# Gate and branch projections moved behind the attention as four stages of seven block products

## The chip, the cores and the metric

The kernel runs on one core of a Trainium2 chip. Its engines have instruction queues of their own: TensorE (PE, with its weight loads PEld), VectorE (DVE), ScalarE (ACT), GpSimd (POOL), and SyncE (SP), which issues most transfers. They meet through semaphores. The metric is the device time of one execution in microseconds, as the median of several runs.

## The reference

One layer on x of 1024 tokens by 1024 channels, in float32. A modulated RMS norm gives h; one combined projection of h feeds two attention branches and the merging gates.

```python
h = rms_norm(x, norm_w[l]) * (1.0 + scale) + shift
hq, hf, hi, hz, gq, gk, gv, gz, ga, mg = jnp.split(h @ w_in[l], IN_OFFSETS, axis=-1)
y_h = hgrn2_branch(hq, hf, hi, hz, ...)   # 8 heads, gated linear attention, rms norm, * silu(hz)
y_g = gla_branch(gq, gk, gv, gz, ga, ...) # 4 heads, the same with other gates
u_h = y_h @ w_branch[l, 0]
u_g = y_g @ w_branch[l, 1]
mg = jax.nn.sigmoid(mg.reshape(B, T, N_BRANCH, D_MODEL))
merged = mg[:, :, 0] * u_h + mg[:, :, 1] * u_g
x = x + gate * (merged @ w_out[l])
return rms_norm(x, final_norm_w)
```

The two halves of `mg`, `u_h` and `u_g` are four products of 1024 x 1024 by 1024 x 1024. They are what the change touches.

## The kernel before

Activations lie transposed, channels on the partitions and the 1024 tokens along the free axis, as eight tiles. For a float32 result every operand is split into two float32r parts, hi and lo, and every product is the sum hi*hi + hi*lo + lo*hi (`split`, L155 on ScalarE and L158 on VectorE). Buffers are 46 slots of 4 KB per partition, given out in program order.

The dense work is a list of jobs. A `Feat` (L422) makes one tile of 128 features for all tokens: 8 channel tiles x 3 parts x 2 token halves = 48 matmuls of 512 columns (`mm_feat`, L414), into one PSUM tile `pd` of 1024 columns; two such tiles take turns. A `Vblk` (L440) makes 256 value features in token layout with 256-column matmuls (L473 to L475). The jobs run in this order: the GLA branch's tiles; then `mg` for u_g and u_g itself (16 Feats; the gated result goes to DRAM, `t1_dram`, L886); the HGRN2 branch's tiles; then `mg` for u_h and u_h itself (16 Feats; L1014 fetches t1 again, L1022 to L1027 multiply and add); then the output projection in token layout (`OutBlk`, L1078 to L1080).

The attention of a head is a generator (`attention`, L487) woven into the jobs. It does a step (small matmuls on TensorE, products of decays on VectorE, copies on ScalarE) and yields the number of dense units, one about six 512-column matmuls, that are to run before its next step. Its score matmuls are L511, L543, L572, L579 and L585, into the PSUM tile `sc_ps`; between them VectorE scales q and k by decays (L591, L592). A root mean over a head or a branch (`root_mean`) sums squares on GpSimd (L791, L965), splits the sum and multiplies it with ones (L769, L770). `Stream.go` runs the jobs and counts units; where a branch product needs a head that is not through, it runs the woven work to its end (`jobs_done`).

After the opening, a list scheduler settles the order within each engine from the program's order. GpSimd issues few transfers, SP the rest.

## Time and profile before

| | |
|---|---|
| median of 3 runs | 1288.39 us (1286.5 to 1289.18) |
| span of the profiled execution | 1287.7 us; the page gives no other time of its own for it |
| TensorE busy | 1254.3 us, 97% |
| VectorE, ScalarE, GpSimd busy | 659.9, 408.8, 89.1 us |
| matmuls (rows) | 9179, of which 3168 are L414 |
| moved by DMA | 86.00 MB, mean 67 GB/s |
| TensorE on the chain that ended last | 61% |

The span is what one execution took from its first to its last instruction. A matmul's row is longer than its share of the time, since the next one starts while it drains; the price of one is read from the starts of neighbours. "Idle before" names what an engine stood still for.

### The profile page before, as it was taken

The page shows a single profiled execution, that of the slowest core. Times are in us where ns is not written, and L with a number is a line of the kernel's source. Part 1 is how long each engine was busy: PE and PEld are TensorE (multiplying, and loading weights), DVE is VectorE, ACT ScalarE, POOL GpSimd, SP SyncE. Part 2 cuts the span into 40 slices and gives each one's busy share as a digit, 9 for nine tenths or more (in the row PEclk, how much of TensorE's full clock was granted, in tenths as well). Part 3 has the DMA queues.
Part 4 walks back from the last instruction along what each step waited for, and adds up shares of the span by engine and source line. Part 5 has one row for each costly group of instructions (what it writes and reads, how often), then busy time and mean ns, then how long its engine had stood idle before and what let it go on. Part 6 is the DMA issues. An engine that isn't in the chain of part 4 may idle for free.

```text
span 1287.7 us, 20979 instructions
## 1 busy us (share of the span) xinstructions
PE 1254.3 (97%) x9179; PEld 1059.2 (82%) x9179; DVE 659.9 (51%) x1053; ACT 408.8 (32%) x606; POOL 89.1 (7%) x104
## 2 busy tenths in 40 slices
PE   4899999999999999999999999999999999999997
PEld 3767889889898888888889879888988888878886
DVE  5736334563837362224564556375466430585534
ACT  4566712333223241112232332333233231222222
POOL 5500000000000000000000000000000000140000
PEclk9799999999999999999999999999999999999999
DMA  8613010202002103363010201020010111333302
GB/s 273 224 33 90 26 34 2 66 2 66 18 19 65 34 17 115 122 211 92 18 34 18 82 2 34 17 83 18 18 50 18 50 50 50 131 98 130 132 33 99
DMA packets 99822, 86.00 MB, mean 67 GB/s; under 512 B 3211, under 2 KB 89281, under 8 KB 99730
## 3 DMA queue, kind: packets, MB, share of 16 engines
q1 hardware_dynamic: 98242, 80.24, 20.2%
q0 software_dynamic: 1440, 4.40, 0.9%
q8 instruction: 72, 1.18, 0.4%
q14 instruction: 20, 0.16, 0.0%
q10 hardware_dynamic: 48, 0.01, 0.0%
HBM read 76.25 MB, written 8.39 MB: 66 GB/s over the span
## 4 chain that ended last, share of the span: by engine, by line
PE 61%; DVE 2%; issue 0%; POOL 0%; ACT 0%; POOLq 0%; DVEq 0%; ACTq 0%
PE pd L414 41%; PE pd L473 2%; PE pd L474 2%; PE pd L475 2%; PE pd L1080 2%; PE pd L1079 2%; PE pd L1078 2%; PE pm L657 1%; PE pm L659 1%; PE pm L640 1%; PE sc_ps L511 1%; PE sc_ps L543 1%; PE pm L621 0%; DVE b L158 0%; PE sc_ps L572 0%
## 5 line engine op out<-in xcount | busy, mean ns | idle before, releaser
L414 PE MATMUL pd<-b,b 128*128 128x512 f32 x3168 | 750.1, 393 | 1.7 <-DVE b L1026 1.7
L414 PEld LDWEIGHTS pd<-b,b 128*128 128x128 f32 x3168 | 587.4, 188 | 125.9 <-DVE b L1026 2.1
L158 DVE TENSOR_TENSOR b<-b,b 128x1024 fp32r<-128x1024 f32 (+1 forms) x143 | 171.8, 1216 | 191.9 <-ACT b L155 112.5
L155 ACT CAST b<-b 128x1024 fp32r<-128x1024 f32 (+1 forms) x143 | 134.6, 955 | 302.8 <-PE pd L414 86.3
L473 PE MATMUL pd<-b,b 128*128 128x256 f32 x512 | 149.6, 292 | 0.0
L475 PE MATMUL pd<-b,b 128*128 128x256 f32 x512 | 144.9, 283 | 0.0
L474 PE MATMUL pd<-b,b 128*128 128x256 f32 x512 | 144.8, 283 | 0.0
L473 PEld LDWEIGHTS pd<-b,b 128*128 128x128 f32 x512 | 98.0, 191 | 1.4
L474 PEld LDWEIGHTS pd<-b,b 128*128 128x128 f32 x512 | 98.1, 192 | 0.5
L475 PEld LDWEIGHTS pd<-b,b 128*128 128x128 f32 x512 | 98.0, 191 | 0.0
L591 DVE TENSOR_TENSOR b<-b,tot 128x512 f32<-128x512 f32 x36 | 24.8, 690 | 71.3 <-PE sc_ps L572 27.5
L1078 PE MATMUL pd<-b,b 128*128 128x512 f32 x128 | 49.8, 389 | 0.0
L1079 PE MATMUL pd<-b,b 128*128 128x512 f32 x128 | 49.8, 389 | 0.0
L1080 PE MATMUL pd<-b,b 128*128 128x512 f32 x128 | 49.8, 389 | 0.0
L965 POOL TENSOR_TENSOR b<-b,b 128x1024 f32<-128x1024 f32 x7 | 17.5, 2495 | 464.8 <-ACT b L954 464.8
L758 ACT ACTIVATE b<-pd 128x1024 f32<-128x1024 f32 x24 | 24.6, 1026 | 73.7 <-PE pd L414 73.7
L657 PE MATMUL pm<-scT,b 128*128 128x128 f32 x256 | 46.8, 274 | 0.0
L646 DVE SCALAR_TENSOR_TENSOR b<-b,tot,pm 128x128 f32<-128x128 f32 (+1 forms) x72 | 28.2, 391 | 31.9 <-PE pm L640 30.3
L659 PE MATMUL pm<-b,b 128*128 128x128 f32 x224 | 43.3, 275 | 0.0
L657 PEld LDWEIGHTS pm<-scT,b 128*128 128x128 f32 x256 | 39.2, 191 | 1.7
L855 ACT ACTIVATE b<-pd 128x1024 f32<-128x1024 f32 x16 | 16.4, 1026 | 73.9 <-PE pd L414 73.9
L759 DVE TENSOR_TENSOR b<-b,pd 128x1024 f32<-128x1024 f32 x24 | 29.2, 1218 | 18.8 <-ACT b L758 18.8
(191 smaller groups left out, 1264.2 us busy)
## 6 DMA issues: line engine op xcount, KB each, us to landing
b<-in_w_in_dram SPq DMA_DIRECT2D x66, 512.0 KB, 3.7
b<-in_x_dram SPq DMA_DIRECT2D x16, 512.0 KB, 5.6
b<-in_ada_w_dram SPq DMA_DIRECT2D x32, 256.0 KB, 5.9
b<-in_w_branch_dram SPq DMA_DIRECT2D x16, 512.0 KB, 4.1
t_dram<-b POOLq DMA_DIRECT2D x8, 512.0 KB, 3.6
b<-in_ada_w_dram SPq DMA_DIRECT2D x8, 512.0 KB, 5.4
b<-t_dram SPq DMA_DIRECT2D x8, 512.0 KB, 4.4
b<-in_w_out_dram SPq DMA_DIRECT2D x8, 512.0 KB, 4.6
```

Source lines behind the costliest of these rows:

```text
L155: i = nc.scalar.copy(hi, src)
L158: (eng or nc.vector).tensor_sub(lo, src, hi.bitcast(F32))
L414: nc.tensor.matmul(ps[0:w, th * 512:(th + 1) * 512], a[:, k, 0:w], b[:, th * 512:(th + 1) * 512], start=(k == 0 and n == 0), stop=(k == KT ...
L473: nc.tensor.matmul(o, lh, hi[:, k % 4, :], start=(k == 0), stop=False)
L474: nc.tensor.matmul(o, lh, lo[:, k % 4, :], start=False, stop=False)
L475: nc.tensor.matmul(o, ll, hi[:, k % 4, :], start=False, stop=(k == KT - 1))
L657: nc.tensor.matmul(o, vch(ch)[:, vh * P:(vh + 1) * P], scT[:, ch, :], start=True, stop=(ch == 0))
L659: nc.tensor.matmul(o, state(ch)[:, vh * P:(vh + 1) * P], q[:, ch * P:(ch + 1) * P], start=False, stop=True)
L759: nc.vector.tensor_mul(s, s, ps)
L1078: nc.tensor.matmul(po, lh, hi[:, k % 2, :], start=(k == 0), stop=False)
L1079: nc.tensor.matmul(po, lh, lo[:, k % 2, :], start=False, stop=False)
L1080: nc.tensor.matmul(po, ll, hi[:, k % 2, :], start=False, stop=(k == KT - 1))
```

## The change

The 32 Feats of the gates and the branches leave the job list. GLA and HGRN2 jobs follow each other, and behind the last of them stand four stages: the gate of u_g, the gate of u_h, u_g and u_h. Each is a product of 1024 x 1024 matrices, worked in *pairs* of neighbouring feature tiles. For a pair, the weights are a 2 x 2 block matrix (channel halves by the two tiles) and the activations another (channel halves by token halves). Its four output blocks come from seven block products instead of eight, by Strassen's scheme in a form that reuses sums. A block product is 4 channel tiles x 3 parts = 12 matmuls of 512 columns (L1242 of the changed kernel). Each stage runs the products in the order 1, 2, 5, 6, 3, 7, 4, each for its four pairs, so a product's activation factor is loaded once per stage; the second stage uses the first one's factors.

The sums and differences that the scheme needs are made beforehand, while the attention runs, and kept in DRAM: of the activations by `factors` (VectorE, L1087), of the weights by `weight_sums` (VectorE, L1118 to L1122), both stored by GpSimd's queue. They run on a second woven track (`back`); the first track's pace is 1.1 steps of attention per unit instead of 1. h, y_g and y_h go to DRAM as well (`put_act`, L227).

Within a pair, partial results stay in PSUM where they can. After a product, ScalarE or VectorE reads the bank: a snapshot into SBUF (L1218, L1220), a finished block (L1229, or the gate's and branch's own step: L1315, L1320 sigmoid, L1330, L1337 product), or ScalarE writes an earlier snapshot into a bank on which the next product accumulates (L1225). The banks are the six 512-column halves of the two `pd` tiles and of `sc_ps`, which is lent when the last head's scores are through (`scores_done`). The last stage adds the stored u_g part with an accumulating DMA (L1340), and `make_m` splits the result for the output projection, which now starts with tokens 512 to 1023.

```diff
-ROOM = 9
-LOOK = 6
+PACE = 1.1
+PRODUCTS = (1, 2, 5, 6, 3, 7, 4)
+SUMS = {5: 0, 6: 1, 3: 2, 7: 3}
+SEEDS = {(6, 2): 0, (6, 3): 1, (3, 0): 2, (3, 1): 3}
...
     def make_h(half, d):
...
+        if d % 2:
+            nc.gpsimd.dma_start(h_d[half][d // 2], hT[half, d // 2].rearrange("p a t -> p (a t)"))
...
         def weave(self, units):
-            entry = self.side[0]
-            entry[1] -= units
...
+            for track, pace in ((self.side, PACE), (self.back, 1)):
+                if not track:
+                    continue
+                entry = track[0]
+                entry[1] -= units * pace
...
+    def put_act(acts, d, y):
+        for half in range(2):
+            nc.gpsimd.dma_start(acts[half][d // 2][:, d % 2 * 512:d % 2 * 512 + 512], y[:, half * 512:half * 512 + 512])
+        S.free(y)
...
-    for d in range(LOOK):
-        J.append(Feat(col(C_MG + D + d * P), rhs_h, mg_done(gate1, d)))
-    for d in range(8):
-        J.append(Feat(w_branch[0, 1, :, d * P:(d + 1) * P], rhs_yg, ug_done(d)))
-        if d + LOOK < 8:
-            J.append(Feat(col(C_MG + D + (d + LOOK) * P), rhs_h, mg_done(gate1, d + LOOK)))
...
-    for d in range(8):
-        J.append(Feat(col(C_MG + d * P), rhs_h, mg0_done(d)))
-    for d in range(8):
-        J.append(Feat(w_branch[0, 0, :, d * P:(d + 1) * P], rhs_yh, uh_done(d)))
...
+    def factors(acts, f, mul=None):
+        sub = nc.vector.tensor_sub
+        for kk in range(2):
...
+            for p, dst, a, b in ((5, "11", "12", "11"), (7, "12", "12", "22"), (6, "22", "22", "11"), (4, "21", "21", "22")):
+                sub(y[dst], y[a], y[b])
+                nc.gpsimd.dma_start(f[p][kk], y[dst])
...
+    def weight_sums(b, i):
...
+        add(parts[7], x1[:, :, 0], x1[:, :, 1])
+        add(parts[5], x1[:, :, 1], x2[:, :, 1])
+        yield 1.5
+        add(parts[6], parts[7], x2[:, :, 1])
+        add(parts[3], parts[6], x2[:, :, 0])
...
+        def run(self, p):
+            if p in (1, 5):
+                self.bank[BANK[p]] = R.get()
+            o = self.bank[BANK[p]]
...
+            for kt in range(4):
+                h_hi, h_lo = (z[kt // 2][:, kt % 2, :] for z in h)
+                sl = slice(kt * P, (kt + 1) * P)
+                for n, (a, c) in enumerate(((hi, h_hi), (hi, h_lo), (lo, h_hi))):
+                    nc.tensor.matmul(o, a[:, sl], c, start=(p in (1, 5) and kt == 0 and n == 0),
+                                     stop=(kt == 3 and n == 2), skip_group_check=True)
...
+        def after(self, p):
+            bank, snap, out = self.bank, self.snap, outs[self.b]
+            if p == 1:
+                snap[1] = self.snap_of("a", -1.0)
+            elif p == 2:
+                out(2 * self.i, 0, bank["a"], False)
+                R.free(bank.pop("a"))
+            elif p == 5:
+                snap[5] = self.snap_of("e")
+                R.free(bank.pop("e"))
+                self.seed("b", snap[1])
+                Q.free(snap.pop(1))
+            elif p == 6:
+                snap[6] = self.snap_of("b", -1.0)
+            elif p == 3:
+                self.summed(0, 1, None, bank["e"], ALU.subtract, 6)
+                R.free(bank.pop("e"))
+            elif p == 7:
+                self.summed(1, 1, bank["b"], None, ALU.add, 5)
+            else:
+                out(2 * self.i + 1, 0, bank["b"], False)
+                R.free(bank.pop("b"))
...
+    def put_m(d, half, ap, summed):
+        sl = slice(half * 512, half * 512 + 512)
+        g = gate0[d][:, sl]
+        nc.vector.tensor_mul(g, g, ap)
+        if summed:
+            Q.free(ap)
+        nc.gpsimd.dma_start(g, gate1[d][:, sl], accum_op=ALU.add)
+        later.append((d, half))
...
     stream.go()
+    S.free(*h_hi, *h_lo)
+    for _ in range(2):
+        pd = dtile()
+        R.lend([pd[:, 0:512], pd[:, 512:1024]])
+    last_stages()
+    make_m()
+    out0.run({1: out1.load, 3: out1.prep})
+    out1.run({})
```

Below, (b, p) names product p of stage b, b from 0 to 3. Three places show how the order moved. On TensorE, between two branch tiles of u_h before (the numbers tell buffers apart; `x2` is the same weights on both token halves):

```order
L414 MATMUL pd_9326<-b_9032,b_9283 128x512 x2
L414 MATMUL pd_9326<-b_9033,b_9283 128x512 x2
L414 MATMUL pd_9326<-b_9032,b_9284 128x512 x2
L414 MATMUL pd_9394<-b_5319,b_9351 128x512 [waits DVE_49,Activation_49]
L414 MATMUL pd_9394<-b_5320,b_9351 128x512 x2
L414 MATMUL pd_9394<-b_5319,b_9352 128x512 x2
```

and in the second stage after, at product (1, 2), where `pd_7871` and `pd_7872` are the two 1024-column tiles, each with two pairs' banks:

```order
L1242 MATMUL pd_7871<-b_7892,b_8735 128x512
L1242 MATMUL pd_7871<-b_7894,b_8735 128x512
L1242 MATMUL pd_7871<-b_7892,b_8736 128x512
L1242 MATMUL pd_7872<-b_8078,b_8771 128x512 [waits Activation_49]
L1242 MATMUL pd_7872<-b_8080,b_8771 128x512
L1242 MATMUL pd_7872<-b_8078,b_8772 128x512 [waits DVE_49]
L1242 MATMUL pd_7872<-b_8078,b_8771 128x512
L1242 MATMUL pd_7871<-b_7891,b_8735 128x512 [waits Activation_49]
L1242 MATMUL pd_7871<-b_7893,b_8735 128x512
```

Before, a tile is read once, after 48 matmuls, while the next 48 fill the other tile. Now a bank is read after 12; four matmuls of another pair stand between the end of one half of `pd_7871` and the start of its other half, which waits for ScalarE's read.

On VectorE, in the fourth GLA head between the steps L572, L579 and L585, before:

```order
L591 TENSOR_TENSOR b_608<-b_608,tot_744 128x32x16
L592 TENSOR_TENSOR b_2628<-b_2628,tot_744 128x32x16
L598 COPY_PREDICATED blk<-mask_735,sc_ps 128x8x16
L591 TENSOR_TENSOR b_608<-b_608,tot_744 128x16x32
L592 TENSOR_TENSOR b_2628<-b_2628,tot_744 128x16x32
L591 TENSOR_TENSOR b_608<-b_608,tot_744 128x8x64
L592 TENSOR_TENSOR b_2628<-b_2628,tot_744 128x8x64
```

and after, where L634 and L635 are the former L591 and L592:

```order
L634 TENSOR_TENSOR b_636<-b_636,tot_776 128x32x16
L635 TENSOR_TENSOR b_2889<-b_2889,tot_776 128x32x16
L641 COPY_PREDICATED blk<-mask_767,sc_ps 128x8x16
L196 TENSOR_TENSOR b_4029<-b_3850,b_4028 128x1024
L1118 TENSOR_TENSOR b_4050<-b_3969 128x512
L1119 TENSOR_TENSOR b_4049<-b_3969,b_3970 128x512
L634 TENSOR_TENSOR b_636<-b_636,tot_776 128x16x32
L635 TENSOR_TENSOR b_2889<-b_2889,tot_776 128x16x32
L1121 TENSOR_TENSOR b_4049<-b_4050,b_3970 128x512
```

Two weight sums and a subtraction of a weight split came between the updates of q and k that TensorE's next scores need.

On ScalarE, while u_h is made before (L155 casts weights, 1024 columns, or the merged result, 512 columns):

```order
L155 CAST b_9419<-b_9324 128x1024 [waits DMAHW2_49]
L155 CAST b_9246<-b_8708 128x512 [waits DVE_49,Pool_49]
L155 CAST b_9246<-b_8708 128x512 [waits DVE_49]
L155 CAST b_9314<-b_8793 128x512 [waits DVE_49,PE_49,Pool_49]
L155 CAST b_9314<-b_8793 128x512 [waits DVE_49]
```

and around products (3, 7) and (3, 4) after (L193 casts the merged result, L1182 weights, L1163 activation factors; DMASW are the transfers that GpSimd issues, here the accumulating ones):

```order
L1220 ACTIVATE b_10060<-sc_ps 128x512 [waits PE_49]
L1225 COPY sc_ps<-b_9937 128x512 [waits Activation_49]
L1225 COPY pd_7872<-b_9980 128x512 [waits DVE_49]
L1225 COPY sc_ps<-b_9980 128x512 [waits DVE_49]
L193 CAST b_9897<-b_8753 128x512 [waits DMASW3_49]
L1182 CAST b_10237<-b_10139 128x1024 [waits DMAHW3_49,DMAHW2_49,PE_49]
L193 CAST b_9915<-b_8769 128x512 [waits DMASW4_49]
L1182 CAST b_10188<-b_10085 128x1024 [waits DMAHW1_49,PE_49]
```

The casts of the merged result waited for VectorE; now they wait for a transfer, with weight casts behind them in ScalarE's queue, and between them stand the reads and seeds of PSUM banks.

More of the change, by code (lines that the diff above doesn't have):

```diff
@@ L691, in go @@
         def go(self, loads=2, preps=1):
+            n = len(self.jobs)
             for i, job in enumerate(self.jobs):
@@ new lines, in half_of, with put_gate1 @@
+    def half_of(store, d, half):
+        if d not in store:
+            store[d] = S.get([T])
+        return store[d][:, half * 512:half * 512 + 512]
+    gate0, gate1 = {}, {}
+    gate1_d = [dp.tile([P, T], F32, name=f"gate1_{d}") for d in range(8)]
+    m_hi, m_lo = [None] * 8, [None] * 8
+    def put_gate1(d, half, ap, summed):
+        g = ap if summed else Q.get()
+        nc.scalar.activation(g, ap, AF.Sigmoid)
+        nc.gpsimd.dma_start(gate1_d[d][:, half * 512:half * 512 + 512], g)
+        Q.free(g)
```

423 lines of the change are left out of this document (301 added, 122 removed).

## The prediction

> **What bounds the kernel now.** I read the page's shares and slices first.
>
> ```profile
> PE 1254.3 (97%) x9179; PEld 1059.2 (82%) x9179; DVE 659.9 (51%) x1053; ACT 408.8 (32%) x606; POOL 89.1 (7%) x104
> ...
> PE   4899999999999999999999999999999999999997
> ...
> PEclk9799999999999999999999999999999999999999
> ```
>
> TensorE is busy in every slice but the first three, at the full granted clock after them. Since a busy row can hide small gaps, I read the waits of TensorE next, and then stretches of 40 us.
>
> ```profile
> PE pm L217 <- DMA b<-in_ada_w_dram: 8.7, 1, 8.7
> ...
> PE pd L414 <- DVE b L1026: 1.7, 1, 1.7
> PE pm L770 <- DVE b L158: 1.3, 1, 1.3
> ```
>
> ```profile
> core 0: us, PE busy (x) PEld busy (x) DVE busy (x) ACT busy (x) POOL busy (x), PEclk, DMA share, GB/s
> 0.00:40.00 40.00, 20.59 (x76) 16.75 (x76) 22.24 (x42) 16.66 (x32) 20.20 (x61) 0.93 0.84 261
> 240.00:280.00 40.00, 40.00 (x422) 33.38 (x421) 35.89 (x62) 16.22 (x24) 0.00 (x0) 1.00 0.10 27
> ...
> 640.00:680.00 40.00, 40.00 (x380) 33.80 (x379) 25.63 (x54) 11.09 (x21) 0.00 (x0) 1.00 0.10 27
> 1080.00:1120.00 40.00, 40.00 (x178) 33.11 (x177) 14.53 (x11) 12.70 (x13) 0.00 (x0) 1.00 0.41 131
> ```
>
> The reader is to see two things. Past the start only two waits are worth naming, 1.7 and 1.3 us. And TensorE stayed full in 240 to 280 us although VectorE was busy for 35.89 of the 40 us. So the time is a count of matmuls times the price of one, and what the change can lose is new waiting of TensorE. The price stands in the output projection, where nothing is woven in:
>
> ```profile
> 1192.64 0.39 PE L1078 MATMUL pd<-b,b 128*128 128x512 f32 x1
> 1192.87 0.39 PE L1079 MATMUL pd<-b,b 128*128 128x512 f32 x1
> ...
> 1204.88 0.39 PE L1078 MATMUL pd<-b,b 128*128 128x512 f32 x1
> 1205.11 0.39 PE L1079 MATMUL pd<-b,b 128*128 128x512 f32 x1
> ```
>
> 1204.88 - 1192.64 = 12.24 us for 54 matmuls: one 512-column matmul costs 0.2267 us, and its 0.39 us row overlaps the next. There the weights change at every matmul, as they will in the new stages.
>
> **The change, part by part.** The base is the profiled execution: span 1287.7 us, 0.7 us under the runs' median of 1288.39; the page shows no time around the span.
>
> *Matmuls.* Before, 32 Feat jobs (gates and branches) take 48 matmuls each, 1536. After, 4 stages x 7 products x 4 pairs x 12 = 1344. The 192 fewer at 0.2267 us are -43.5 us, on the path, since TensorE is full there.
>
> *Old waits.* L1026 (1.7) and L770 (1.3) wait for flushes that are gone: -3.0 us.
>
> *Hand-overs.* Each of the 112 pair products ends in a read or seeding of its bank by ScalarE or VectorE. The length of one is seen where the attention's output leaves PSUM:
>
> ```profile
> 446.39 0.39 PE L659 MATMUL pm<-b,b 128*128 128x128 f32 x2
> ...
> 446.53 1.63 PE L414 MATMUL pd<-b,b 128*128 128x512 f32 x6
> 446.81 0.60 ACT L785 ACTIVATE b<-pm 128x512 f32<-128x512 f32 x1 [2.36 <-PE pm L659]
> ```
>
> The next matmul takes its slot at 446.53; the bank has been read at 446.81 + 0.60 = 447.41, so 0.88 us later, 3.9 slots. The changed order has 32 waits of TensorE for such a read with fewer than 12 matmuls between (mostly 4, 0.91 us); in all 32 the bank read is the other half of the 1024-column tile that TensorE writes next. Four slots just cover 0.88 us if the reading engine is free. What it may be doing instead:
>
> ```profile
> L158 DVE TENSOR_TENSOR b<-b,b 128x1024 fp32r<-128x1024 f32 x111 | 143.3, 1300 | 181.2 <-ACT b L155 102.0 <-PE pd L414 27.8 <-PE pd L475 17.2
> L155 ACT CAST b<-b 128x1024 fp32r<-128x1024 f32 x111 | 115.7, 1051 | 246.8 <-PE pd L414 86.3 <-PE pd L475 24.2 <-PE pd L474 22.8
> L1084 DVE TENSOR_TENSOR b<-b,xb 128x512 f32<-128x512 f32 x16 | 11.1, 692 | 0.5
> ```
>
> A stage takes 336 x 0.2267 = 76 us and holds 28 casts of 1.05 us (14 weights, 14 activations), so a cast is running 39% of the time, with 0.53 us of it left on average: 0.2 us per wait. I take 32 x 0.2 = +6.4; the ends are 0 (every cast falls elsewhere) and 32 x 1.05 = 33.6. The very first hand-over of the stages and the last of the output projection have nothing between: +1.8.
>
> The Trainium skill (PSUM — Partial Sum Buffer, Terms) names the bank of 2 KiB as the unit that two engines may not use at once. By that rule a half is free while its neighbour is read, the 32 waits guard nothing, and a program without them would come out 6.4 us lower; this program carries them, and no run yet shows it without.
>
> *Attention.* Gates no longer run beside it, and a pace of 1.1 takes a tenth off the dense work between its steps. The margin before:
>
> ```profile
> 657.94 0.46 PE L579 MATMUL sc_ps<-b,b 128*32 128x32 f32 x32
> ...
> 658.33 3.02 PE L414 MATMUL pd<-b,b 128*128 128x512 f32 x12
> ...
> 659.34 0.69 DVE L592 TENSOR_TENSOR b<-b,tot 128x512 f32<-128x512 f32 x1
> ...
> 661.28 0.69 PE L585 MATMUL sc_ps<-b,b 128*64 128x64 f32 x16
> ```
>
> VectorE was ready at 660.03, TensorE came at 661.28: 1.25 us to spare, under 2.7 us of dense work. In the fourth GLA head the changed order has 1.6 us there, and two weight sums (0.69 each by L1084's row) ahead of the update: 1.25 - 1.1 - 1.4 is 1.2 us late. Such insertions stand at twelve tight steps, 22 sums and four differences (1.3 us by L158's row): 20 us if all are exposed, 0 if none. I take 5, nearer to none, since TensorE stayed full beside a VectorE at 90% (240 to 280 us). The densest phase is GLA's four heads:
>
> ```profile
> 160.00:440.00 280.00, 280.00 (x2546) 246.65 (x2545) 148.24 (x255) 84.10 (x124) 7.49 (x3) 1.00 0.12 33
> ```
>
> VectorE's 148 us of 280 (53%) become 148 + 64 x 0.69 + 8 x 1.3 = 202 in 280 / 1.1 = 254, or 80%.
>
> *Last root mean.* It now stands in the first stage, with 19 slots (4.3 us) from the last attention matmul. GpSimd's addition, the square, the cast and the subtraction:
>
> ```profile
> L965 POOL TENSOR_TENSOR b<-b,b 128x1024 f32<-128x1024 f32 x7 | 17.5, 2495 | 464.8 <-ACT b L954 464.8
> ```
>
> 0.6 + 2.5 + 1.05 + 1.3 + 0.25 for hops = 5.7: +1.4, between 0 (if a later matmul is moved ahead) and 4 (GpSimd first issues queued stores).
>
> *DMA.* The program's own DMAs go from 84.6 to 197.9 MB, 327 from SP (181 before) and 175 from GpSimd (17 before). GpSimd's were few, and this is what they took:
>
> ```profile
> L886 POOL DMA_DIRECT2D t_dram<-b x8: 533/533/597, 485.1 to 575.3; - x8
> ...
> DMA to landing us min/median/max: 2.9/4.1/6.8
> ```
>
> Issuing 158 more at 0.53 us is 84 us of GpSimd beside a span of idling, so 0 on the path. SP's loads are issued 61 to 130 slots (14 to 29 us) ahead of their matmuls, so a landing of 4 to 7 us, a cast and a subtraction fit. In the densest 57 us of the first two stages 21.3 MB are issued; 261 GB/s at a share of 0.84 means 311 at full share, 17.7 MB, a backlog of 3.6 MB or 12 us. The lead covers most: +1, ends 0 and 5. In the last stage ScalarE's casts wait for an accumulating DMA, with casts that TensorE needs queued behind. At (3,4) the path is 0.69 + landing + 0.62 + 1.05 + 1.3 against 37 slots (8.4 us): late by -1.8 to 2.1 us with landings of 2.9 to 6.8. A second such place: +1.5 for both, ends 0 and 4.
>
> The Trainium skill's SBUF — State Buffer page (the "DVE blocks DMA" trap) says that a POOL-issued DMA starves while VectorE holds the shared port, 3.1 against 0.62 us in its example. The 2.9 to 6.8 spread agrees in kind, but no row here tells that cause from others. By it each accumulating DMA lands 2.5 us later, an estimate from that page, and the sum would be some 5 us higher.
>
> *Start.* The eight stores of h cost GpSimd 0.53 us each; TensorE's first 353 rows stand as before: 0.
>
> The sum: 1287.7 - 43.5 - 3.0 + 6.4 + 1.8 + 5 + 1.4 + 1 + 1.5 = 1258.3, so 1258.
>
> **The rivals.**
> - *The cover is complete.* All terms but the 1.8 vanish: 1287.7 - 46.5 + 1.8 = 1243. For it: no steady wait appears before. Against: 39% casts in a stage.
> - *Late engines.* The attention's steps are late by 0.5 us in each of 12 heads x 6 steps, or the DMA backlog shows: 1243 + 36 = 1279. For it: VectorE at 80% with thinner gaps. Against: 240 to 280 us.
> - *The hand-overs are bare (slower).* If each pair product stops TensorE for the whole 0.88 us, 112 x 0.88 = 98.6, so 1287.7 - 46.5 + 98.6 = 1340. It decides from 46.5 / 112 = 0.42 us per hand-over. For it: 32 waits between half tiles, and in-order engines loaded by two thirds. Against: the 23 other waits of that kind and the 9 on one bank have 12 or more matmuls between.
> - *Nothing comes of it.* Waits of 44 to 49 us just eat the gain: 1288.
>
> **How the numbers follow.** The forecast's case (1249 to 1270) 0.55; complete cover 0.20; late engines 0.11; bare hand-overs 0.11; nothing 0.03. The forecast is 1258. From 1243 to 1282 lie the first case, half of the second and most of the third. A measurement of this kernel tells some 0.2% (2.6 us) from no change; faster by more: 0.55 + 0.20 + 0.11 = 0.86; same 0.02; slower 0.12, with 0.01 of the nothing case.
>
> **What would show it.** Right: 8987 matmul rows (192 fewer), windows in the stages with some 44 matmuls per 10 us, small PE waits on L1220, L1315, L1320, L1330 and L1337, none above 3 us, clock 1.00. Wrong: PE waits above 20 us in total on VectorE's L634, L635 and L691 (attention), or for factor and weight casts behind a DMA; a fall of the stages' rate below 38 per 10 us (1344 in 305 + 46.5 us), at which the gain is gone.

## The result, and the profile after

The changed kernel takes 1295.64 us (median; 1292.4 to 1297.65) against 1288.29 us of the kernel before: a ratio of 1.0060, 95% interval 1.0038 to 1.0081. It is 0.6% slower, where 1258 was forecast. Its profiled execution took 1292.4 us, with a span of 1290.7.

The page's shares and slices, after:

```profile
PE 1227.4 (95%) x8987; PEld 1025.7 (79%) x8987; DVE 791.7 (61%) x1223; ACT 505.9 (39%) x754; POOL 158.9 (12%) x254
...
PE   4899999999999989999999999989889999998997
...
PEclk9799999999999999999999999999999999998999
```

The 192 matmuls are gone (8987 rows). But TensorE's idle time in the span rose from 33.4 us (1287.7 - 1254.3) to 63.3 us, and its busy time fell by 26.9 us only, mostly since the clock was lower at times: its mean over the execution is 0.983, against 0.992 before, and 0.009 of 1290 us are some 12 us. Its waits, past the start:

```profile
PE pd L1242 <- ACT b L1182: 5.1, 1, 5.1
PE pd L1242 <- ACT b L1220: 4.8, 3, 2.9
...
PE pm L916 <- DVE b L909: 3.6, 1, 3.6
PE pm L818 <- DVE b L196: 3.5, 5, 0.8
PE pd L1242 <- DVE b L1229: 3.4, 2, 2.6
PE pd L1025 <- DVE xb L1030: 3.1, 2, 2.3
```

They are few and long, not many and short: single places, not a toll on each of the 112 hand-overs. Three of them, each in the time line of the engines (start, us, engine, line). At 930 us, in the first stage:

```profile
929.65 0.70 PE L1242 MATMUL pd<-b,b 128*128 128x512 f32 x2 [2.63 <-DVE b L1229]
```

```profile
923.02 1.23 DVE L1081 TENSOR_TENSOR b<-b,b 128x1024 f32<-128x1024 f32 x1 [1.34 <-DMA b<-yh]
927.68 1.22 DVE L1081 TENSOR_TENSOR b<-b,b 128x1024 f32<-128x1024 f32 x1 [3.42 <-DMA b<-yh]
928.82 0.68 DVE L1229 TENSOR_TENSOR b<-pd,b 128x512 f32<-128x512 f32 x1
```

VectorE stood 3.42 us at a load of y_h, for the factors that only the fourth stage needs, with the read of a bank (L1229) behind it that TensorE needed now. At 1162 us, in the fourth stage:

```profile
1163.18 0.62 ACT L193 CAST b<-b 128x512 fp32r<-128x512 f32 x1 [8.02 <-DMA b<-b]
1163.70 1.04 ACT L1182 CAST b<-b 128x1024 fp32r<-128x1024 f32 x1
```

ScalarE stood 8.02 us at an accumulating DMA, with a cast of weights behind it; TensorE waited 5.1 us. At 475 us, the gate of the output, whose eight loads came late (VectorE's L909 waits 2.51 us and 0.77 us for them), TensorE waited 3.6 us. What the wait does to the clock stands in the windows around it (columns as in the prediction):

```profile
475.00:480.00 5.00, 1.44 (x5) 0.40 (x3) 5.00 (x8) 1.04 (x1) 0.70 (x2) 0.97 0.59 176
480.00:485.00 5.00, 5.00 (x6) 1.50 (x6) 4.79 (x7) 0.58 (x1) 0.38 (x1) 0.50 0.43 147
485.00:490.00 5.00, 5.00 (x69) 3.12 (x68) 1.80 (x3) 1.51 (x3) 0.54 (x1) 0.50 0.17 63
490.00:500.00 10.00, 10.00 (x104) 8.06 (x104) 9.85 (x22) 3.94 (x4) 1.78 (x3) 1.00 0.37 133
```

For 10 us behind a wait of 3.6 us the granted clock was 0.50. That costs some 5 us (10 us at half the rate), more than the wait itself. The Trainium skill (TensorE: Matmul & The Clock Gate, What's actually happening) says that the clock is halved after an idle window of about 3.4 us and restored after a busy one. The trace agrees on the half; the clock was back only after 10 us of work.

For the experiments the span is cut in three by the starts of rows: the *attention* from the first L455 (126.0 us) to the first L1242, the *stages* from there to the first L1025, the *output* from there to the last L1027, the last matmul of all:

```profile
L1242 PE MATMUL pd<-b,b x912: 386/389/797, 844.1 to 1187.2; 128*128 128x512 f32 x183
...
L1025 PE MATMUL pd<-b,b x88: 388/389/628, 1190.2 to 1282.1; 128*128 128x512 f32 x88
L1027 PE MATMUL pd<-b,b x88: 387/389/629, 1191.1 to 1282.5; 128*128 128x512 f32 x88
```

718.1, 346.1 and 92.3 us. The same three for every kernel, from its profiled execution, beside its median time and the ratio to the kernel before on the same chip. A profiled execution lies up to 5 us from the median (e4: 1287.3 against 1292.4). One of e6's five executions took 2428 us and one of the kernel before on that chip 1564 us; the ratios leave them out.

| kernel | us | ratio, 95% interval | attention | stages | output |
|---|---|---|---|---|---|
| changed | 1295.64 | 1.0060 (1.0038 to 1.0081) | 718.1 | 346.1 | 92.3 |
| e1_no_accum | 1292.69 | 1.0042 (1.0027 to 1.0057) | 718.1 | 346.1 | 89.3 |
| e2_yh_later | 1299.05 | 1.0092 (1.0071 to 1.0112) | 718.7 | 348.0 | 90.7 |
| e3_gate_loads | 1294.23 | 1.0047 (1.0033 to 1.0060) | 716.1 | 345.4 | 92.8 |
| e4_three | 1292.35 | 1.0044 (1.0031 to 1.0056) | 715.3 | 348.7 | 89.2 |
| e5_no_prep | 1273.01 | 0.9885 (0.9871 to 0.9900) | 708.4 | 336.3 | 92.5 |
| e6_spread | 1293.37 | 1.0053 (1.0040 to 1.0067) | 714.2 | 350.8 | 91.1 |
| e7_all | 1290.19 | 1.0024 (1.0009 to 1.0038) | 710.4 | 354.7 | 88.3 |
| e8_floor | 1260.00 | 0.9790 (0.9776 to 0.9804) | 703.5 | 332.1 | 88.3 |
| e9_gpsimd | 1291.06 | 1.0035 (1.0024 to 1.0047) | 713.0 | 351.2 | 88.3 |
| e10_no_yh | 1285.93 | 0.9986 (0.9976 to 0.9996) | 718.9 | 338.2 | 92.3 |
| e11_no_sums | 1291.25 | 1.0034 (1.0021 to 1.0047) | 710.4 | 349.9 | 90.8 |
| e12_scale_late | 1286.96 | 1.0006 (0.9993 to 1.0019) | 720.1 | 341.2 | 88.3 |
| e13_traffic | 1296.72 | 1.0081 (1.0062 to 1.0100) | 718.8 | 347.3 | 92.4 |
| e14_compute | 1285.14 | 0.9988 (0.9978 to 0.9998) | 719.1 | 336.4 | 90.6 |
| e15_slots44 | 1316.49 | 1.0209 (1.0182 to 1.0237) | 728.8 | 357.0 | 96.3 |
| e16_combined | 1274.80 | 0.9896 (0.9881 to 0.9911) | 709.2 | 339.2 | 88.3 |
| e17_two_slots | 1290.72 | 1.0023 (1.0014 to 1.0033) | 719.8 | 340.1 | 94.0 |

### The profile page after: what moved, and what is told of

Its sections match the earlier page's. It is cut to its first block, busy times and chain, and to the rows that moved or that the text cites. A ratio compares the mean times of both kernels' runs of the same rounds, so it can differ in the third digit from the quotient of the medians.

```text
span 1290.7 us, 21711 instructions
## 1 busy us (share of the span) xinstructions
PE 1227.4 (95%) x8987; PEld 1025.7 (79%) x8987; DVE 791.7 (61%) x1223; ACT 505.9 (39%) x754; POOL 158.9 (12%) x254
## 5 line engine op out<-in xcount | busy, mean ns | idle before, releaser
L455 PE MATMUL pd<-b,b 128*128 128x512 f32 x1632 | 395.9, 396 | 0.0
L455 PEld LDWEIGHTS pd<-b,b 128*128 128x128 f32 x1632 | 301.0, 188 | 62.9 <-issue 0.7
L1242 PE MATMUL pd<-b,b 128*128 128x512 f32 x912 | 223.1, 398 | 17.7 <-ACT b L1182 5.1
L1242 PEld LDWEIGHTS pd<-b,b 128*128 128x128 f32 x912 | 171.4, 191 | 60.8 <-ACT b L1220 7.0
L196 DVE TENSOR_TENSOR b<-b,b 128x1024 fp32r<-128x1024 f32 (+1 forms) x95 | 105.4, 1122 | 81.9 <-ACT b L193 53.5
L193 ACT CAST b<-b 128x1024 fp32r<-128x1024 f32 (+1 forms) x95 | 84.7, 905 | 157.4 <-DMA b<-b 25.4
L1242 PE MATMUL sc_ps<-b,b 128*128 128x512 f32 x432 | 106.8, 393 | 0.1
L1183 DVE TENSOR_TENSOR b<-b,b 128x1024 fp32r<-128x1024 f32 x56 | 67.7, 1219 | 51.5 <-ACT b L1182 34.9
L514 PEld LDWEIGHTS pd<-b,b 128*128 128x128 f32 x512 | 98.1, 192 | 1.3
L515 PEld LDWEIGHTS pd<-b,b 128*128 128x128 f32 x512 | 98.1, 192 | 0.7
L516 PEld LDWEIGHTS pd<-b,b 128*128 128x128 f32 x512 | 98.0, 191 | 0.1
L1242 PEld LDWEIGHTS sc_ps<-b,b 128*128 128x128 f32 x432 | 80.7, 189 | 18.3 <-DVE b L1330 0.5
L1182 ACT CAST b<-b 128x1024 fp32r<-128x1024 f32 x56 | 58.1, 1049 | 41.1 <-DMA gate<-b 8.4
L1164 DVE TENSOR_TENSOR b<-b,b 128x1024 fp32r<-128x1024 f32 x36 | 43.7, 1220 | 35.7 <-ACT b L1163 23.2
L1124 POOL DMA_DIRECT2D ws<-b x64 | 34.7, 543 | 165.5 <-DVE b L1119 70.8
L1163 ACT CAST b<-b 128x1024 fp32r<-128x1024 f32 x36 | 37.7, 1049 | 41.5 <-PE pd L1242 10.1
L634 DVE TENSOR_TENSOR b<-b,tot 128x512 f32<-128x512 f32 x36 | 24.9, 691 | 34.3 <-PE sc_ps L615 15.0
```

What stands on the lines that cost most here:

```text
L193: i = nc.scalar.copy(hi, src)
L196: (eng or nc.vector).tensor_sub(lo, src, hi.bitcast(F32))
L455: nc.tensor.matmul(ps[0:w, th * 512:(th + 1) * 512], a[:, k, 0:w], b[:, th * 512:(th + 1) * 512], start=(k == 0 and n == 0), stop=(k == KT ...
L514: nc.tensor.matmul(o, lh, hi[:, k % 4, :], start=(k == 0), stop=False)
L515: nc.tensor.matmul(o, lh, lo[:, k % 4, :], start=False, stop=False)
L516: nc.tensor.matmul(o, ll, hi[:, k % 4, :], start=False, stop=(k == KT - 1))
```

## The experiments

The theory at first: the time goes where an engine that takes its work in order stands at a late transfer, with work behind it that TensorE needs. The rivals: the hand-overs of banks are bare; VectorE has too much to do; the DMA rate itself is the bound.

### Three places mended, one by one and together

```diff
# e1_no_accum
-        nc.gpsimd.dma_start(g, gate1[d][:, sl], accum_op=ALU.add)
+        nc.gpsimd.tensor_add(g, g, gate1[d][:, sl])
# e2_yh_later
-            stream.back.append([factors(yh_d, f_h, rst), 1])
+            stream.back.append([factors(yh_d, f_h, rst), 60])
# e3_gate_loads (in gate_side)
-            b = S.get([D])
-            nc.sync.dma_start(b, ada_w[0, k * P:(k + 1) * P, 2 * D:3 * D])
+            if k < KT:
+                bs.append(S.get([D]))
+                nc.sync.dma_start(bs[-1], ada_w[0, k * P:(k + 1) * P, 2 * D:3 * D])
+            k -= 3
...
+            b = bs.popleft()
```

> In the last stage GpSimd adds the stored u_g part in SBUF instead of the accumulating DMA; the result is the same. Late transfers: the 8.0 us in which ScalarE stood at the accumulating DMA go, with TensorE's waits of 5.1 and 0.9 us at 1161 and 1182 us, the lower clock behind them (0.79 and 0.87 over 20 us, 3 us) and perhaps the 2.3 us at 1207 us: 1283 to 1287, from 1295.6. Bare hand-overs: the reads of the banks are as before, so 1294 to 1297. VectorE overloaded: its work is unchanged, so 1294 to 1297.

> The scaling of y_h and its factors begin 60 units after the last root mean instead of 1, so behind the first stage. Late transfers: VectorE no longer stands 10.0 us at loads of y_h with the bank reads L1229 and the weight subtractions L1183 behind it; TensorE's waits of 0.8, 2.6, 0.3, 0.7 and 2.9 us between 919 and 956 us shrink to under 2, with the clock of 0.83 behind them: 1286 to 1289, from 1295.6. Bare hand-overs: the waits stay, with other names, 1293 to 1297. DMA rate itself the bound: the same bytes move later and TensorE waits there instead, 1293 to 1297.

> The eight ada_w loads of the output gate are issued three steps ahead of their use. Late transfers: TensorE's wait of 3.6 us at L916 and the granted clock of 0.50 in the 10 us behind it (5 us lost) go: 1286 to 1289, from 1295.6. VectorE overloaded: L909 is late because of its own queue, so the wait stays or moves to the next attention step, 1293 to 1297.

> The three edits together. Late transfers, if the three places are independent: -10, -8 and -8 from 1295.6, so about 1270, and between 1266 and 1275. Each rival: 1290 or more. If the time lost only moves to the next transfer, the sum falls short of the three single gains by more than 6 us.

Measured: 1292.69, 1299.05, 1294.23 and together 1292.35 us, where the theory wanted 1270 of the last. Each named wait went from its place, and the time with it did not: all four intervals overlap that of the changed kernel. e2 alone has an even longer median. In e4 TensorE no longer stands in the first stage from 890 us on, so no hand-over stops it there; and then, in the second, where the work on y_h now stands (L1250 is the former L1242, L1089 the former L1081, L1237 the former L1229):

```profile
984.39 0.84 PE L1250 MATMUL sc_ps<-b,b 128*128 128x512 f32 x3
992.62 3.54 PE L1250 MATMUL pd<-b,b 128*128 128x512 f32 x8 [7.39 <-ACT pd L1233]
```

```profile
988.96 1.23 DVE L1089 TENSOR_TENSOR b<-b,b 128x1024 f32<-128x1024 f32 x1 [9.12 <-DMA b<-yh]
990.10 0.68 DVE L1237 TENSOR_TENSOR b<-b,pd 128x512 f32<-128x512 f32 x1
```

It is the same kind of wait, longer, 60 units later: VectorE at a load of y_h, behind it the read of a bank, behind that ScalarE's seed of the bank. In e1 the 8.02 us of ScalarE went, but GpSimd's additions slowed VectorE's subtractions beside them from 0.68 to as much as 1.77 us, and were slowed themselves from 1.28 to 2.15:

```profile
1172.32 2.15 POOL L1340 TENSOR_TENSOR b<-b,b 128x512 f32<-128x512 f32 x1 [1.82 <-DMA b<-in_w_branch_dram]
```

```profile
1173.25 1.77 DVE L196 TENSOR_TENSOR b<-b,b 128x512 fp32r<-128x512 f32 x1
```

In e3 the wait of 3.6 us at L916 is gone, and one of 3.2 us at L615 has come 30 us later, behind six weight sums within 6 us on VectorE, which had stood 4.84 us at a load of weights just before. So these are places where time is lost, but not what it is lost to.

### What is left without the preparation

e5 takes all preparation of sums out; e8 also has the gate loads of e3, and VectorE instead of the accumulating DMA.

```diff
-    stream.back.append([prepare(), 60])
...
-            stream.back.append([factors(yg_d, f_g), 4])
...
-            stream.back.append([factors(yh_d, f_h, rst), 1])
...
-    w_sums = [[[dp.tile([P, T], F32, name=f"ws{b}{j}{i}") for i in range(4)] for j in range(2)] for b in range(4)]
+    w_sums = [h_d for b in range(4)]
# e8 also
-        nc.gpsimd.dma_start(g, gate1[d][:, sl], accum_op=ALU.add)
+        nc.vector.tensor_add(g, g, gate1[d][:, sl])
```

> All the work that prepares sums is left out (the 16 weight sums, the factors of h, y_g and y_h with their scaling): the stages load unprepared blocks of the same size in their place, so the output is not the reference's. 1344 matmuls, their order, the hand-overs of banks, the stores of the gate and the accumulating DMA stay. If the preparation is what makes engines late (VectorE's sums between the attention's steps, loads and stores that VectorE and ScalarE stand at), the attention phase gets some 10 us shorter and the stages some 15, and what is left is the accumulating DMA and the end: 1262 to 1270, from 1295.6. Bare hand-overs: 1285 or more. A matmul price that is higher in the stages: 1285 or more.

> As e5, so with an output that is not the reference's, and also with the gate loads of e3 and VectorE adding u_g. This is the matmul count with next to no late transfer. If hand-overs are covered: 1247 to 1256, the prediction's sum without its terms for DMA and attention. If hand-overs cost the 0.2 us each that the prediction took: 6 us more. Bare: above 1280.

Measured: 1273.01 and 1260.00 us, 3 and 4 us above their ranges. Windows of e8's first two stages:

```profile
900.00:920.00 20.00, 20.00 (x89) 16.23 (x88) 8.36 (x11) 7.41 (x11) 3.78 (x7) 1.00 0.59 183
920.00:940.00 20.00, 20.00 (x89) 16.38 (x88) 6.06 (x5) 9.42 (x14) 1.62 (x3) 1.00 0.51 172
```

89 matmuls in 20 us are 0.225 us each: the price holds, with every hand-over in place. TensorE's waits in e8 for bank work (L1225 reads a bank, L1230 seeds one, L1335 is u_g's product, L1320 the gate), and for a weight subtraction (L1188):

```profile
PE pd L1247 <- DVE b L1188: 2.8, 1, 2.8
...
PE pd L1247 <- ACT b L1225: 1.8, 1, 1.8
...
PE pd L1247 <- ACT pd L1230: 1.1, 1, 1.1
PE sc_ps L1247 <- DVE b L1335: 0.8, 1, 0.8
...
PE pd L1247 <- ACT b L1320: 0.2, 1, 0.2
```

1.8 + 1.1 + 0.8 + 0.2 = 3.9 us for 112 hand-overs. The rival of the bare hand-overs (98.6 us) is refuted. e8 itself lies 16 us above the prediction's complete cover (1259.2 against 1243): TensorE still waits 11.4 us past the start, these 3.9 among them, and the clock behind the 2.8 us wait (0.66 and 0.65 over 1150 to 1160 us) takes 3.4. The preparation and the three places cost 1290.7 - 1259.2 = 31.5 us of span: 14.6 in the attention, 14.0 in the stages, 4.0 in the output, less a start that was 1.2 us later in e8's execution.

### The preparation spread out, and put on another engine

e6 only spreads the weight sums over the attention. e7 adds the gate loads, later and longer leads for the factors, and VectorE for the last addition. e9 puts the y_h work on GpSimd.

```diff
# e6_spread, in weight_sums
-        yield 6
+        yield 12
...
-        yield 3
+        yield 6
# e7_all also, in factors; e2's 60 is 30 here
-            yield 6
+            yield 14
# e9_gpsimd also, in factors
-        sub = nc.vector.tensor_sub
+        eng = nc.vector if mul is None else nc.gpsimd
+        sub = eng.tensor_sub
```

> Only the pace of the weight sums: 12 units instead of 6 between their loads and their first addition, 6 instead of 3 behind each, so they fill all of the attention instead of its first 60 per cent, with longer leads. Late loads and crowded steps: the 3.6 us wait and low clock at L916 and the small waits of the GLA phase shrink, 4 to 10 us, 1286 to 1292. If the sums cost by their mere number on VectorE: 1294 to 1297.

> The pace of e6, the gate loads of e3, factors of y_h 30 units later, 14 instead of 6 units between the loads of any factor and its first use, and VectorE instead of an accumulating DMA adding u_g. Late transfers: no in-order engine stands at a transfer any more, so most of the 35 us come back: 1262 to 1272, from 1295.6. If the time lost only moves to the next transfer, as in the three edits together: 1284 to 1292.

> As e7 (weight sums at a pace of 10 and 5 units), with the factors of y_g between the weight sums of the second and third stage instead of behind them all, and the scaling and differences of y_h on GpSimd, behind which nobody that TensorE needs is queued. The result is the same. VectorE standing at loads and stores of the factors is the cost: the stages take 332 to 338 us (354.7 in e7, 332.0 in e8) and the attention stays at about 710 us, so 1265 to 1274. The DMA rate or the slots are the cost, whoever does the work: stages of 348 or more, 1284 or more. GpSimd slows VectorE (0.68 to 1.77 us beside its additions in e1) so far that the gain is eaten: 1276 to 1284.

Measured: 1293.37, 1290.19 and 1291.06 us. Spreading shortens the attention, by 3.9 us in e6 and 7.7 in e7. But the stages get longer, to 354.7 us in e7, where VectorE stood at loads of y_h in spite of the lead, and at stores of the factors, since a difference is written over a tile whose store has to land first:

```profile
DVE b L1089 <- DMA b<-yh: 14.2, 5, 4.5
...
DVE b L1095 <- DMA fh<-b: 8.7, 2, 6.3
```

In e9 it is GpSimd that stands, 25.1 us at once, and not without harm: the stores of the gate are issued by GpSimd too, and ScalarE waits for the buffers that they hold. GpSimd's waits, then a row of ScalarE's:

```profile
POOL gate L1331 <- ACT b L1330: 71.6, 10, 28.7
POOL b L1091 <- DMA b<-yh: 30.7, 3, 25.1
```

```profile
ACT b L1197 <- DMA gate<-b: 7.1, 2, 6.7
```

A load that is 25 us late in spite of 14 units of lead (84 matmuls, 19 us) is not slow in its transfer (in the changed kernel the transfers of y_h, stores and loads, land in 2.3 to 7.4 us). It is issued late. SyncE's waits in the changed kernel between 895 and 960 us show at what:

```profile
SPq L1075 <- DMA fh<-b: 9.2, 2, 8.3
...
SPq L1171 <- DMA fh<-b: 7.8, 1, 7.8
SPq L1175 <- DMA gate<-b: 6.5, 1, 6.5
...
SPq L1075 <- DMA gate<-b: 6.2, 1, 6.2
```

A load needs a slot, and the slot next in turn is still held by a store that has not landed; SyncE takes its loads in order, so every load behind stands too. Of 50.7 us of such waits in these 65 us, 29.7 are for stores; the other 21.0 are for operands in a slot that are not used up yet. So the theory got a second part: the slots.

A slot can also stop a bank read with no load between. At 955 us ScalarE stood 4.26 us because the slot for its snapshot was still held by a store of the gate, and TensorE stood for that snapshot:

```profile
955.22 0.60 ACT L1220 ACTIVATE b<-pd 128x512 f32<-128x512 f32 x1 [4.26 <-DMA gate<-b]
```

```profile
955.87 1.43 PE L1242 MATMUL pd<-b,b 128*128 128x512 f32 x5 [2.86 <-ACT b L1220]
```

Counted in the order of the products, the matmul belongs to the fourth pair of product (1, 1) and the snapshot to the third pair, whose bank is a different one. Of the 11.4 us that TensorE waits for bank work in the changed kernel's stages (L1220, L1229, L1337, L1225, L1315), 10.0 us stand like this, at another pair's bank; only the 1.4 us at L1225 are for the matmul's own. These are the waits between half tiles that the prediction counted. Half of all that TensorE waits in the stages (20.2 us) reaches it through them, and no kernel without them was run.

### Which part of the preparation costs

e10 leaves out the y_h factors, e11 the weight sums. e13 keeps y_h's loads and stores and drops VectorE's operations, e14 the reverse.

```diff
# e10_no_yh
-            stream.back.append([factors(yh_d, f_h, rst), 1])
+            S.free(rst)
# e11_no_sums, in prepare
-        for b in range(4):
-            for i in range(4):
-                yield from weight_sums(b, i)
# e13_traffic, in factors
-                    nc.vector.tensor_mul(v, v, mul[:, half * 512:half * 512 + 512].unsqueeze(1).to_broadcast([P, 2, 512]))
...
-                sub(y[dst], y[a], y[b])
+                if mul is None:
+                    sub(y[dst], y[a], y[b])
# e14_compute, in factors
-                nc.sync.dma_start(y[b], part_of(acts, int(b[0]) - 1, int(b[1]) - 1, kk))
+                if mul is None:
+                    nc.sync.dma_start(y[b], part_of(acts, int(b[0]) - 1, int(b[1]) - 1, kk))
```

> The changed kernel, only without the factors of y_h: the last stage loads unscaled blocks of y_h, so the output is not the reference's. Late transfers in front of VectorE: TensorE's waits between 919 and 956 us go, -8 to -11, so 1284 to 1288 from 1295.6. If e2 showed that this work costs nothing but moves: 1292 or more.

> The changed kernel, only without the weight sums: the stages load blocks of h of the same size in their place, so the output is not the reference's. If the sums on VectorE and their loads and stores make the attention late: its 717.8 us become 706 to 710 and the 3.6 us wait at L916 with its slow clock goes, 1284 to 1288. If they are covered: 1293 to 1297.

> The changed kernel, with the loads and stores of the y_h factors but none of VectorE's 16 operations on them, so its output is not the reference's. Transfers and the slots that they hold are the cost: most of the 9.7 us between 1295.6 and the 1285.9 of e10 stay, 1292 to 1296. VectorE standing at them is the cost: 1285 to 1289.

> The reverse of e13: VectorE's 16 operations for the y_h factors on its own slots, with no loads before and no stores behind them; the last stage loads unscaled blocks of y_h, so the output is not the reference's. VectorE's time itself (20 us) is the cost: 1292 to 1296. Standing at transfers is the cost, and VectorE has the time: 1285 to 1289.

Measured: 1285.93 without y_h's factors, 1291.25 without weight sums, 1296.72 with the traffic alone, 1285.14 with the computing alone. Windows of 920 to 960 us, first e13, then e14:

```profile
920.00:940.00 20.00, 17.30 (x68) 13.56 (x67) 7.64 (x10) 8.16 (x11) 2.71 (x5) 0.91 0.68 223
940.00:960.00 20.00, 19.81 (x86) 15.62 (x84) 4.69 (x6) 7.59 (x11) 4.84 (x9) 1.00 0.81 285
```

```profile
920.00:940.00 20.00, 20.00 (x89) 16.40 (x89) 18.64 (x20) 8.87 (x12) 4.87 (x9) 1.00 0.60 196
940.00:960.00 20.00, 20.00 (x90) 16.23 (x89) 6.76 (x6) 11.01 (x15) 0.54 (x1) 1.00 0.57 178
```

In e14 VectorE is busy for 18.64 of 20 us and TensorE is full; in e13 VectorE has time and TensorE does not. That refutes the overloaded VectorE in the stages: without its transfers the work on y_h costs nothing.

e13 shows less than its time says. Without the scaling, the stores of y_h's factors no longer wait for the last root mean, and one of them stood in GpSimd's queue ahead of that root mean's addition (L961), which the changed kernel makes at 884.72 us:

```profile
892.56 0.54 POOL L1082 DMA_DIRECT2D fh<-b  x1 [8.01 <-DMA b<-yh]
893.64 2.35 POOL L961 TENSOR_TENSOR b<-b,b 128x1024 f32<-128x1024 f32 x1
```

```profile
897.12 1.11 PE L817 MATMUL pm<-b,ones_r 128*128 128x512 f32 x2 [4.99 <-ACT b L193]
```

This wait and the clock behind it (0.73 over 895 to 900 us and 0.93 over the next 5: 1.7 us) are 6.7 of the 11.6 us between e13 and e14, at a place where the changed kernel waits 1.0 us. Another 2.7 us of wait and 1.7 us of clock stand at 924 us, at the seed of a bank, before which ScalarE stood 4.25 us at a load of h's factors. In e14 TensorE is full there. So the traffic of y_h makes another load late with no work of VectorE between, and that is some 4.4 us. Whether the rest of the 9.7 us needs VectorE standing at the loads is not shown.

### Slots

e15 has 44 slots instead of 46. e17 lends two more, for plain loads and scratch, from the first stage on: 8 KB of the attention's score buffer.

```diff
# e15_slots44
-N_SLOTS = 46
+N_SLOTS = 44
# e17_two_slots, in scores_done
         R.lend([sc_ps[:, 0:512], sc_ps[:, 512:1024]])
+        S.lend([xb_f[:, 0:1024], xb_f[:, 1024:2048]])
```

> The changed kernel with 44 slots instead of 46, nothing else; 47 don't fit. SyncE's loads standing in order at slots that stores or matmuls still hold is the bound of the stages: they get longer by 4 us or more, 1299 to 1306, from 1295.6. The DMA rate or VectorE is: 1293 to 1298.

> The changed kernel, only with the two slots lent from the first stage on. e15 took two slots away in all of the program and its stages grew by 10.9 us. Slots are the bound of the stages: they shrink from 346.1 us to 337 to 342, so 1286 to 1292 from 1295.6. If the two slots only hurt where they were missed in the attention: 346, 1294 to 1297.

Measured: 1316.49 and 1290.72 us. With the same bytes, two slots fewer cost 20.9 us by the medians (e15's four executions took 1307.8 to 1318.1), more than either theory expected, half of it in the attention (10.7 us). But e15 also moves work: `factors` and `weight_sums` start only when eight or six slots are free, so the second half of h's factors ran at 236 to 251 us instead of 189 to 193, and y_g's at 585 to 632 instead of 535 to 565. Its price is not that of standing loads alone. e17 leaves the order before the stages nearly as it was (it also gives the output projection's scratch to the slots; its output is 1.7 us longer). Two more slots took 6.0 us from the stages and 4.9 from the median. So the DMA rate alone is not the bound. It has a share that stays open: in 920 to 940 us of the changed kernel the DMA engines' share is 1.01, and e17 still loses time there:

```profile
920.00:940.00 20.00, 16.43 (x63) 12.77 (x64) 9.43 (x10) 6.13 (x8) 5.20 (x11) 0.91 1.01 348
```

```profile
920.00:940.00 20.00, 16.54 (x67) 13.06 (x66) 13.10 (x14) 5.61 (x8) 5.34 (x11) 0.91 0.95 338
```

(The changed kernel, then e17.) How much of the 9.7 us of the y_h traffic is full DMA engines and how much slots was not told apart.

### A form with less to move

A factor per token can be multiplied in behind the product. So y_h stays unscaled in its stage and its root mean goes into the gate of u_h; eight scalings and six stores fall away. e12 has this with e7's other edits at a denser pace (8 and 4), and half of y_h's differences beside the attention. e16 has a pace of 10 and 5, all of y_h's differences from the second stage on, y_g's ahead of the last stage's weight sums, and the two lent slots.

```diff
-    f_x, f_g, f_h = new_factors(h_d, "fx", False), new_factors(yg_d, "fg", False), new_factors(yh_d, "fh", True)
+    f_x, f_g, f_h = new_factors(h_d, "fx", False), new_factors(yg_d, "fg", False), new_factors(yh_d, "fh", False)
...
-        nc.scalar.activation(half_of(gate0, d, half), ap, AF.Sigmoid)
+        g = half_of(gate0, d, half)
+        nc.scalar.activation(g, ap, AF.Sigmoid)
+        nc.vector.tensor_mul(g, g, rst_h[0][:, half * 512:half * 512 + 512])
```

> Pace 8 and 4 units for the weight sums, the gate loads of e3, the factors of y_g in between as in e9, VectorE adding u_g, and y_h kept unscaled: its root mean is multiplied into the gate of u_h in the second stage (16 products of 512 columns on VectorE), since a factor per token may as well be applied behind the product. The eight scalings and six scaled stores of y_h go, and half of its differences are made beside the attention, after head 5. The result is the same up to rounding. If work that waits for transfers in front of VectorE is the cost: stages of 336 to 342 us (346.1 in the changed kernel, 332.1 in e8), attention 708 to 713, out 88: 1268 to 1278. If any work put there costs as much as it did: 1285 to 1291.

> e12 with a pace of 10 and 5 units for the weight sums, the factors of y_g ahead of the last stage's weight sums, all of y_h's differences in one piece from the second stage on, and two more slots for plain loads from the first stage on: the attention's score buffer xb (10 KB), which is done by then, lends 8 KB, and the output projection takes its scratch from the slots. The result is the same. Slots held by transfers are the bound: stages of 333 to 337 us (341.2 in e12), attention 711 to 715 (713.0 in e9, 720.1 in e12), out 88: 1270 to 1277, under the kernel before. Not the bound: stages of 340 or more, 1280 to 1287.

Measured: 1286.96 and 1274.80 us. e12's stages came down to 341.2 us, but its attention to no less than 720.1, with denser weight sums and half of y_h's differences in it; which of the two costs was not told apart. e16 beats both kernels: 0.9896 of the kernel before, interval 0.9881 to 0.9911. Its stages missed the expected 333 to 337 us. Its page:

```profile
PE 1221.0 (96%) x8987; PEld 1023.8 (80%) x8987; DVE 801.9 (63%) x1247; ACT 506.7 (40%) x754; POOL 139.5 (11%) x232
```

VectorE is busier than in the changed kernel, and the time is 20.8 us shorter.

## Why the prediction was wrong

The chance of faster was put at 0.86, and the time lies outside the range of 1243 to 1282. Step by step:

- **Matmuls, -43.5: right.** 8987 rows; 89 in 20 us in every undisturbed window of the stages.
- **Old waits, -3.0: half right.** The wait of L1026 is gone. The other, of a root mean (L770, now L818), is not: it stands five times in the list, for 3.5 us where it was 1.3.
- **Hand-overs, +6.4 and +1.8: right in kind, a little too high.** In e8, where little else is late, 3.9 us; 1.8 of them are the very first hand-over, which the prediction counted apart, so 2.1 stand against the 6.4, and 1.8 with 0.8 in the output against the 1.8. In the changed kernel the waits at another pair's bank are 10.0 us, the first hand-over again among them, because reads come late; the prediction had taken only a cast in front of a read, not a transfer. No kernel without the 32 other-half waits was run, so the rule of the Trainium skill on banks (PSUM — Partial Sum Buffer, Terms) stays untested, and what those waits cost with late transfers stays open.
- **Attention, +5 with ends of 0 and 20: mis-sized, and for the wrong places.** It is 14.6 us (718.1 against 703.5 in e8), of which 7.7 go without the weight sums (e11). The 20 us end was nearer. But for VectorE's updates of q and k (L634, L635), which the prediction priced, TensorE waits 0.3 us in all. The largest single piece (3.6 us and 5 us of clock at L916) is at a place that the prediction did not look at (so are 2.8 us at four root means of GLA heads): the side work of the output gate, whose loads now share the DMA engines with those of the sums (a share of 1.06 in 470 to 475 us). Without the weight sums, in e11, the wait there is 1.65 us.
- **Last root mean, +1.4: about right.** TensorE's waits there are 0.8 us (L818, at 889 us) and 0.2 us (L817).
- **DMA, +1 and +1.5 with ends of 0 to 5 and 0 to 4: this step failed.** "SP's loads are issued 61 to 130 slots (14 to 29 us) ahead of their matmuls, so a landing of 4 to 7 us, a cast and a subtraction fit" reads the lead from the order. On the chip SyncE could not issue them then: the slots that they were to fill were held by stores still in flight, or by operands not used yet, and loads that had a slot stood behind those that had none. The work on y_h costs 9.7 us (e10), all of which goes with its transfers (e14); how much of that is slots and how much full DMA engines stays open. The accumulating DMA costs 8.4 us (from e5 to e8 the stages fall by 4.2 us and the output by 4.2). The price of a landing was too low as well: the accumulating DMAs landed in 3.3 to 9.7 us, not 2.9 to 6.8.
- **GpSimd's issues, 0: right as such,** no wait in the list is for one. What the prediction left out is that each store it issues holds a slot until it lands.
- **The clock, not in the sum.** The prediction asked for 1.00. After some waits of 2.3 us and more TensorE ran at a lower clock for some microseconds. At 475 us that cost more than the wait. In all it is 11.8 us: 5.0 at 480 to 490 us, 1.7 at 930 to 935 (0.66), 3.4 at 1165 to 1175 (0.58 and 0.74) and 1.7 at 1210 to 1215 (0.66).

Put together: past the start TensorE waits 33.1 us and loses 11.8 to the clock, where the sum had 17.1 for everything. 1287.7 - 43.5 - 3.0 + 33.1 + 11.8 = 1286.1 of the measured 1290.7; the other 4.6 us are not placed. The signs of being wrong would not have told it: the waits named there stay at 0.3 us in the attention and 6.2 us for casts of weights (L1182, L1183), and the stages still run 38.8 matmuls per 10 us (1344 in 346.1 us). The signs of being right did: waits of 5.1 and 3.6 us, and a clock that was not 1.00.

Of the rivals, *complete cover* (1243) fell, *late engines or the DMA backlog* (1279, chance 0.11) came nearest to the mechanism, late transfers, though by a backlog of bytes and not by slots, with a price of 36 us above complete cover where the measured sum is 52 (1295.6 - 1243). *Bare hand-overs* (1340), the only case of the slower side with a chance worth naming, is refuted; the kernel is slower by another way. *Nothing* (1288) came nearest to the number. The Trainium skill's SBUF — State Buffer page, by which POOL-issued DMAs starve while VectorE holds the shared port, was given 5 us; accumulating DMAs did land late, but at DMA shares of 0.80 (1160 to 1180 us) and 0.98 (1180 to 1200 us), so no run tells its cause from plain load.

## What to carry to other kernels

A change that trades matmuls for transfers has to be counted in buffers first: a slot that was stored from is not free until the store has landed, and one queue that takes loads in order passes each such delay on to all loads behind it. Lead read from the program order is not lead; ask which transfer the buffer of each load has to wait for. And where single waits move instead of vanishing when mended one by one, take the whole suspected work away once (here e8, then e14): that tells in two runs what four repairs did not. Then look where the time went in the trace, since an edit that takes work away lets other work move (e13, e15).

## What was not expected of the hardware

- **Short waits lower the clock too.** The 2.3 us wait at 1207 us in the changed kernel was followed by a granted clock of 0.66 over 5 us, the wait of 2.86 us at 953 us by none. In e1 even a wait of 1.8 us, which ended at 851 us, was followed by 0.70 over 850 to 855. The windows behind the first:

```profile
1210.00:1215.00 5.00, 5.00 (x15) 3.98 (x16) 1.28 (x2) 0.72 (x2) 0.00 (x0) 0.66 0.00 0
1215.00:1220.00 5.00, 5.00 (x23) 4.13 (x22) 1.85 (x3) 0.72 (x2) 0.00 (x0) 1.00 0.00 0
```

  The 3.4 us of the Trainium skill (TensorE: Matmul & The Clock Gate, What's actually happening) is no safe bound here. That page has the window run freely of the kernel, which would explain why like waits end differently; no run here shows it.
- **Half the bytes landed no sooner.** The gate's stores of 256 KB landed in 2.3 to 7.2 us, 4.7 in the median; GpSimd's stores of 512 KB in the kernel before, in 2.9 to 6.8, 3.6 in the median. The changed kernel's DMA share was 0.82 over 895 to 960 us, that of the kernel before 0.26 to 0.43 over 480 to 560.
- **GpSimd beside VectorE.** Additions of 128x512 float32 on GpSimd took VectorE's subtractions from 0.68 to between 1.39 and 1.77 us (e1), though GpSimd was all but idle otherwise. The rows shown read like taking turns: the addition ends at 1174.47 us, the subtraction, begun at 1173.25, at 1175.02.
- **Two slots of 46, 4% of the buffers, are worth 20.9 us** in e15, 1.6% of the time, with the work that moves with them.
